# First block's gates: eight of sixteen column blocks computed with the tokens stationary, then turned

## The chip, the cores and the metric

The kernel runs on one core of one Trainium2 chip. The metric is device time in microseconds for one launch, as the median of several runs. The times shown were taken on one chip, and the profile is one further execution on it.

## The reference, cut to what matters

Two transformer blocks follow each other on a sequence of 256 tokens with 2048 features, in float32. The change touches the gate of the first block's attention.

```python
def swa_sink_mixer(h, w_in, sinks):
    q, k, v, z = split(h @ w_in, [2048, 2304, 2560])   # 2048 | 256 | 256 | 2048 columns
    ...                                               # windowed attention with sinks, 32 heads of 64
    return o, z

def first_block(x, ...):
    h = rmsnorm(x, g_pre)
    o, z = swa_sink_mixer(h, w_in_a, sinks_a)
    y = (o * silu(z)) @ w_out_a
    return x + rmsnorm(y, g_post)

def second_block(x, ...):      # MLA and differential attention, a merge, an FFN, three norms
    ...
```

The gate is `silu(z)`, with z the last 2048 columns of `h @ w_in_a`.

## The kernel before, in words

**Weights.** All matrices are cut into 128 x 128 tiles and stored in the order in which they are used, 16 tiles to a chunk of 1 MB. `Weights.load` (L54) fetches a chunk on SyncE's queue into one of four `w_raw` buffers. `Weights.cut` splits 8 tiles at a time into a high part `w_hi` (ScalarE, L85) and a low part `w_lo` (VectorE, L86), each with four buffers. A product is the sum hi·hi + hi·lo + lo·hi.

**Two ways of multiplying.** `gemm` (L330) takes one block of 128 output columns. The weight tile is stationary. For each of the 16 tiles along the 2048 features there is one matmul of the high weights with the activation's high and low halves side by side (512 columns moving), and one of the low weights with the high half (256 columns moving). The result has features on the partitions and tokens along the free axis. `gemm_nat` (L389) takes 512 output columns, four weight tiles at a time. A block of 128 tokens is stationary, and the weights move: for each of the 16 steps and each of two token blocks there are three matmuls of 512 columns. The result has tokens on the partitions.

**Turning.** Where a result with tokens on the partitions is wanted with features there, `turned` (L450) has VectorE transpose 32 x 32 blocks (L453), and `moved` (L441) then issues 16 DMAs of 16 KB (L446) that bring the blocks to their partitions, from GpSimd's queue (POOL) unless told otherwise. Weights are stored with columns permuted (`_quarters`) so that this works out.

**First block.** K and V are computed first, then 16 blocks of queries by `gemm`, then 16 blocks of gates, each a `gemm` (L640 to L650). A gate block j becomes `g[j]` in these steps: total on ScalarE and VectorE (L419, L212), times the norm's factor (L212), tanh (ScalarE, L646), z(1 + tanh) (VectorE, L647), 0.5 of it times the attention's output `o_a` (VectorE, L636), and the split into halves (ScalarE, L245, and VectorE, L246). The output projection `out_a` follows: three runs of `gemm_nat` (L681), which take `g[0]`, `g[1]`, ... in order, and four blocks one at a time.

**Attention beside it.** The 16 pairs of heads are worked on beside these products by generators in `between`, an `Interleave`. After every 8 weight tiles it has a tick, and each tick lets one generator go on to its next `yield`; a generator names how many ticks it waits. The first active one that is due goes first, and a queued one starts only when no active one is due. `attention_a` uses two ticks in three: at one it issues the values of pair i - 3 (`values_a`, on PE, with a bank `ps_t`) and the scores of pair i (`ps_s`), and two ticks later the transposes and DMA moves of the probabilities (`turned_probs`: twelve pieces on POOL, four on SyncE, `prob_t<-prob_tr`). Afterwards it has one free tick in three. Between the program's order and the engines' own order stands a scheduler that places instructions of each engine, so that weight cuts run ahead of the matmuls.

After `out_a`, a norm over its result (`rstd` on POOL, L708) stands between the first block and the second.

Of the kernel before, what the change touches and what calls it, by code (L numbers as in the profile page):

```python
# [10 lines left out]
F32R = mybir.dt.float32r  # L11
AF = mybir.ActivationFunctionType
ALU = mybir.AluOpType

P = 128
# [156 lines left out]
def block_kernel(ctx, tc, order, w, x01, xt, bc, rw, cst, out):  # L172
    nc = tc.nc
# [11 lines left out]
    between = Interleave()  # L185

    def unit(name, dt=F32):
        return up.tile([P, 512], dt, name=name, tag="u", bufs=NU)
# [7 lines left out]
    def sm(name, n=4):  # L196
        return small.tile([P, n], F32, name=name, tag="sm", bufs=16)

    def bank(tag):
        return psum.tile([P, 512], F32, name=f"ps_{tag}", tag=tag, bufs={"g": 4, "s": 2, "t": 2}[tag])  # L200

    def half(t, i):
        return t[:, (i % 2) * S:(i % 2) * S + S]
# [37 lines left out]
    def split_scaled(src, g, hl):  # L241

        hi = hl[:, 0:S]
        if g is None:
            a = nc.scalar.copy(out=hi, in_=src)  # L245
            b = nc.vector.tensor_tensor(out=hl[:, S:], in0=src, in1=hi.bitcast(F32), op=ALU.subtract)  # L246
        else:
            a = nc.scalar.activation(out=hi, in_=src, func=AF.Copy, scale=g)
            b = nc.vector.scalar_tensor_tensor(out=hl[:, S:], in0=src, scalar=g, in1=hi.bitcast(F32),
                                               op0=ALU.mult, op1=ALU.subtract)  # L250
        return a, b
# [78 lines left out]
    def gemm(name, m, acts, tag="g"):  # L330

        ps = bank(tag)
        parts = [(ps, W.take(name, k * P, m * P), acts[k]) for k in range(len(acts))]
        if len(parts) > HALF:
            runs(parts[:HALF], parts[HALF:], HALF)
        else:
            runs(parts, [], len(parts))
        return ps
# [19 lines left out]
    def gemm_sum(name, m, acts):  # L358

        kind[0] = "hi"  # L360
        ps = bank("g")
        n = len(acts)
        for k in range(n):
            hi, lo = W.take(name, k * P, m * P)
            mm(ps[:, 0:S], hi, acts[k][:, 0:S], k == 0, False)
            mm(ps[:, 0:S], hi, acts[k][:, S:], False, False)
            mm(ps[:, 0:S], lo, acts[k][:, 0:S], False, k == n - 1)
            between.tiles(1)
        return ps
# [31 lines left out]
    def gemm_nats(name, cols, acts, late):  # L401

        banks = [[bank("g") for _ in range(2)] for _ in cols]
        n = len(acts)
        kind[0] = "hi"
        for ks in (range(late), range(late, n)):
            for col, pp in zip(cols, banks):
                for k in ks:
                    while acts[k] is None:
                        between.tick()  # L410
                    hi, lo = W.take(name, k * P, col, 4)
                    for tb in range(2):
                        nat3(pp[tb], acts[k], tb, hi, lo, k == 0, k == n - 1)
                    between.tiles(4)
        return banks
# [6 lines left out]
    def scaled(o, ps, rb):  # L422
        total(o, ps)
        tt(o, o, rb, ALU.mult)
# [71 lines left out]
    h = Lazy(KD, first_h)  # L496
# [8 lines left out]
    for k in range(KD):  # L505
        if k % 2 == 0:
            h.upto(k + 4)
        parts = [(ps_k[j], W.take("in_a", k * P, D + j * P), h[k]) for j in range(2)]
# [9 lines left out]
    r_a = const.tile([P, 2], F32, name="r_a")  # L518
# [80 lines left out]
    done = set()  # L599
    between.every, between.apart = 4, 1  # L600
    between.add(first_norm())
    o_a = []
    early = []
    for j in range(16):
        ps = gemm("in_a", j, h, "s" if j == 2 else "g")
# [7 lines left out]
        for i, b in early:  # L613
            if i % 2 == 0:
                q, o = unit("q_a"), unit("o_a")
# [10 lines left out]
                            axis=mybir.AxisListType.X)  # L626
# [2 lines left out]
    tt(neglam, dots[:, 1:2], dots[:, 0:1], ALU.subtract)  # L629
    nc.vector.tensor_scalar(out=neglam, in0=neglam, scalar1=0.2, scalar2=None, op0=ALU.subtract)  # L630

    g = []

    def gate_a(j, z):
        hl = unit(f"g{j}", F32R)
        nc.vector.scalar_tensor_tensor(out=z, in0=z, scalar=0.5, in1=half(o_a[j // 2], j), op0=ALU.mult, op1=ALU.mult)  # L636
        split_scaled(z, None, hl)
        g.append(hl)

    for j in range(16):  # L640
        ps = gemm("in_a", 20 + j, h)
        if j % 2 == 0:
            z2, th2 = unit("z"), unit("th")
        z, th = half(z2, j), half(th2, j)
        scaled(z, ps, rb)
        nc.scalar.activation(out=th, in_=z, func=AF.Tanh, scale=0.5)  # L646
        nc.vector.scalar_tensor_tensor(out=z, in0=th, scalar=1.0, in1=z, op0=ALU.add, op1=ALU.mult)  # L647
        while j not in done:
            between.tick()
        gate_a(j, z)  # L650
    between.drain()


# [25 lines left out]
    for i in range(3):  # L679
        parts = []  # L680
# [9 lines left out]
    for m in range(12, 15):  # L690
        ps = gemm("out_a", m, g)
        t = y[m]
# [3 lines left out]
    t = sm("ms_y", 2)  # L696
    for tb in range(2):
        nc.vector.tensor_reduce(out=t[:, tb:tb + 1], in_=sums_y[:, 3 * tb:3 * tb + 3], op=ALU.add,
                                axis=mybir.AxisListType.X)
    nc.vector.tensor_scalar(out=t, in0=t, scalar1=1.0 / D, scalar2=EPS, op0=ALU.mult, op1=ALU.add)  # L700
    ps = gemm_sum("out_a", 15, g)
# [31 lines left out]
    h = Lazy(KD, second_h)  # L733
# [53 lines left out]
    ps = gemm("kpe", 0, h)  # L787
# [71 lines left out]
    for u in range(4):  # L859
        kn = []  # L860
        for i in range(4):
            ps = gemm("uk", 4 * u + i, ckv)
# [9 lines left out]
        for tb in range(2):  # L872
            t = unit("v_m")
# [6 lines left out]
        for i in range(4):  # L880
            ps = gemm("uq", 4 * u + i, cq)
# [140 lines left out]
    for u in range(4):  # L1022
        qk = []
        for c in (0, 16):
            parts = []
            for tb, ps in enumerate(gemm_nat("dqk", (c + 4 * u) * P, h)):
                z = unit("qk_d")
# [8 lines left out]
        for tb in range(2):  # L1036
# [3 lines left out]
                                           op0=ALU.mult, op1=ALU.subtract)  # L1040
# [24 lines left out]
    pairs = gemm_nats("diff", [0, 512], y_d, 8)  # L1065
# [11 lines left out]
    h = [None] * KD  # L1077
# [20 lines left out]
    for tb in range(2):  # L1098
        nc.vector.tensor_reduce(out=ms[:, tb:tb + 1], in_=sums3[:, 4 * tb:4 * tb + 4], op=ALU.add,
                                axis=mybir.AxisListType.X)  # L1100
# [5 lines left out]
    for u in range(KF // 4):  # L1106
# [5 lines left out]
        parts = []  # L1112
        for tb, ps in enumerate(pg):
            z = unit("ffn")
# [21 lines left out]
    for cb in range(3):  # L1136
        for tb, ps in enumerate(gemm_nat("down", cb * 512, act)):
            residual(cb, tb, ps)
            t = x2n[2 * cb + tb]
# [12 lines left out]
    for tb in range(2):  # L1152
        nc.vector.tensor_reduce(out=ms3[:, tb:tb + 1], in_=tot[:, 5 * tb:5 * tb + 3], op=ALU.add,
                                axis=mybir.AxisListType.X)
# [3 lines left out]
    for tb in range(2):  # L1158
        parts = [(slice(0, 512), pp[0])]
        if tb:  # L1160
            parts = [(slice(0, 256), bank("s")), (slice(256, 512), bank("s"))]
        for i, (cols, ps) in enumerate(parts):
# [3 lines left out]
            if i + 1 < len(parts):  # L1166
                nc.vector.scalar_tensor_tensor(out=ms3[:, tb:tb + 1], in0=tot[:, 5 * tb + 3:5 * tb + 4],
                                               scalar=1.0 / D, in1=ms3[:, tb:tb + 1], op0=ALU.mult, op1=ALU.add)
        r = sm("rms", 1)
        nc.scalar.activation(out=r, in_=tot[:, 5 * tb + 2 + len(parts):5 * tb + 3 + len(parts)], func=AF.Sqrt,  # L1170
                             scale=1.0 / D, bias=ms3[:, tb:tb + 1])
        nc.vector.reciprocal(out=r, in_=r)
        for cb in range(4):
            t = x2n[2 * cb + tb]
# [35 lines left out]
def _quarters(n):  # L1210

    return np.arange(n).reshape(-1, 4, 4, 32).transpose(0, 2, 1, 3).reshape(-1)
# [6 lines left out]
def _matrices(i):  # L1219

    pairs = []
    for j in range(16):
        kt = j // 8
        for hd in (16 * kt + j % 8, 16 * kt + 8 + j % 8):
            pairs.extend(range(hd * 64, hd * 64 + 64))
    pairs = np.array(pairs)
    in_a, in_2 = i["w_in_a"][0], i["w_in_2"][0]
    uq = i["w_uq_2"][0].reshape(768, 16, 192)
    ukv = i["w_ukv_2"][0].reshape(512, 16, 256)
    kpe = in_2[:, 1280:1344]  # L1230
    ffn = np.concatenate([i["w_ffn_gate_2"][0], i["w_ffn_up_2"][0]], axis=1)[:, _quarters(2 * DFF)]
    return {
        "in_a": np.concatenate([in_a[:, :2048][:, pairs], in_a[:, 2048:2560], in_a[:, 2560:][:, pairs]], axis=1),
        "out_a": i["w_out_a"][0][pairs][:, np.concatenate([_quarters(1536), np.arange(1536, 2048)])],
        "in_2": in_2[:, :1280],
        "kpe": np.concatenate([kpe, kpe], axis=1),
        "dqk": in_2[:, 1344:5440][:, _quarters(2 * D)],
        "dv": in_2[:, 5440:7488],
        "gate": in_2[:, 7488:][:, _quarters(2 * D)],
        "uq": np.concatenate([uq[:, :, :128].reshape(768, -1), uq[:, :, 128:].reshape(768, -1)], axis=1),  # L1240
        "uk": ukv[:, :, :128].reshape(512, -1),
        "uv": ukv[:, :, 128:].reshape(512, -1),
        "mla": i["w_mla_proj_2"][0][:, _quarters(D)],
        "diff": i["w_diff_proj_2"][0][:, _quarters(D)],
        "out": i["w_out_2"][0][:, _quarters(D)],
        "ffn": ffn,
        "down": i["w_ffn_down_2"][0][:, _quarters(D)],
    }
# [36 lines left out]
```

## Time and profile before

| | us |
|---|---|
| median of 3 runs | 1968.07 (1968.05 to 1968.17) |
| profiled execution | 1968.4 |
| its span in the trace | 1966.6 |
| gates: first matmul to the start of `out_a` | 134.7 to 239.75 |
| three `gemm_nat` runs of `out_a` | 239.75 to 305.0 |
| PE busy over the span | 1954.7 (99%) |
| VectorE busy | 1227.4 (62%) |
| ScalarE busy | 1009.2 (51%) |
| POOL busy | 636.4 (32%) |

PE is the matrix engine's matmuls, PEld its weight loads, DVE is VectorE, ACT is ScalarE, POOL is GpSimd, SP is SyncE. L12 is line 12 of the kernel. A row of a tile's view gives an instruction with its count, then the shortest, the median and the longest duration in ns, then when the first and the last of them start. A row of the chain or the timeline gives the start and the duration in us. The idle time in front of an instruction stands in brackets with what ended it.

### The profile page before, as it was taken

To read this page: it belongs to the slowest core of one execution; us is meant where nothing else is said; L and a number is where in the kernel's file an instruction comes from. 1 tells how busy PE (TensorE), PEld (TensorE's weight loads), DVE (VectorE), ACT (ScalarE), POOL (GpSimd) and SP (SyncE) were. 2 spreads that over 40 slices of the span, in tenths; PEclk is the share of its full clock that TensorE was granted. 3 is DMA by queue.
4 is the path that set the end of the run, shared out by engine and by line. 5 is a ranking of instruction groups with operands and counts; after the bars stand their busy time and mean duration, and the time that the engine had idled before them with its cause. 6 is when DMAs were issued, how large, how long until landed. Compare 5 with 4: busy or idle time off the path is not lost.

```text
span 1966.6 us, 27298 instructions
## 1 busy us (share of the span) xinstructions
PE 1954.7 (99%) x9404; PEld 1631.3 (83%) x9404; DVE 1227.4 (62%) x1897; ACT 1009.2 (51%) x1588; POOL 636.4 (32%) x1291
## 2 busy tenths in 40 slices
PE   9999999999999999999999999999999999999998
PEld 8888888888888888888888888888888888888887
DVE  7889855888756655556666566655555555545454
ACT  6677655756545544455564344544444444444443
POOL 0555244013362532445622455323332222220000
PEclk9999999999999999999999999999999999999999
DMA  8565565445565665656566665655665555565553
GB/s 306 186 207 198 188 224 182 171 158 178 192 210 191 211 222 203 215 193 216 189 234 217 211 212 194 245 206 192 209 223 206 201 205 203 204 224 193 193 192 107
DMA packets 114491, 398.94 MB, mean 203 GB/s; under 512 B 32880, under 2 KB 66288, under 8 KB 71216
## 3 DMA queue, kind: packets, MB, share of 16 engines
q1 hardware_dynamic: 72096, 370.24, 53.3%
q0 software_dynamic: 41104, 24.99, 4.7%
q10 hardware_dynamic: 1152, 1.97, 0.3%
q8 instruction: 74, 1.21, 0.2%
q14 instruction: 65, 0.53, 0.1%
HBM read 364.03 MB, written 2.10 MB: 186 GB/s over the span
## 4 chain that ended last, share of the span: by engine, by line
PE 95%; DMA 2%; issue 1%; DVE 1%; POOL 1%; ACT 0%; DVEq 0%; POOLq 0%
PE ps_g L209 90%; PE ps_s L209 4%; DMA turned<-turn 2%; PE ps_t L209 2%; POOL turned L446 0%; PE ps_warm L230 0%; DVE w_lo L86 0%; DVE rope_t L212 0%; POOL rstd L290 0%; ACT x1n L1181 0%; DVE q_r L212 0%; DVE y L719 0%; DVE y L718 0%; POOL rstd L708 0%; DVE turn L453 0%
## 5 line engine op out<-in xcount | busy, mean ns | idle before, releaser
L86 DVE TENSOR_TENSOR w_lo<-w_raw,w_hi 128x1024 fp32r<-128x1024 f32 (+1 forms) x677 | 821.8, 1217 | 622.5 <-ACT w_hi L85 619.2
L85 ACT CAST w_hi<-w_raw 128x1024 fp32r<-128x1024 f32 (+1 forms) x677 | 707.4, 1048 | 772.0 <-PE ps_g L209 743.4
L446 POOL DMA_DIRECT2D turned<-turn x744 | 365.3, 498 | 618.6 <-DVE turn L453 339.0
L209 PE MATMUL ps_g<-w_hi,t_lo 128*128 128x512 f32 x1176 | 457.6, 389 | 0.0
L209 PE MATMUL ps_g<-w_lo,t_hi 128*128 128x512 f32 x1176 | 457.5, 389 | 0.0
L209 PE MATMUL ps_g<-w_hi,t_hi 128*128 128x512 f32 x1176 | 457.5, 389 | 0.0
L209 PE MATMUL ps_g<-w_hi,h 128*128 128x512 f32 x1280 | 400.6, 391 | 0.0
L209 PEld LDWEIGHTS ps_g<-w_hi,h 128*128 128x128 f32 x1280 | 240.4, 188 | 50.5 <-issue 0.3
L209 PEld LDWEIGHTS ps_g<-w_hi,t_lo 128*128 128x128 f32 x1176 | 220.8, 188 | 46.0 <-DVE t_lo L212 0.3
L209 PEld LDWEIGHTS ps_g<-w_lo,t_hi 128*128 128x128 f32 x1176 | 220.8, 188 | 45.9
L209 PEld LDWEIGHTS ps_g<-w_hi,t_hi 128*128 128x128 f32 x1176 | 220.8, 188 | 45.6
L209 PE MATMUL ps_g<-w_lo,h 128*128 128x512 f32 x640 | 249.1, 389 | 0.0
L446 POOL DMA_DIRECT2D prob_t<-prob_tr x336 | 165.3, 500 | 199.8 <-DVE prob_tr L461 105.3
L209 PE MATMUL ps_g<-h,w_hi 128*128 128x512 f32 x648 | 160.0, 394 | 0.0
L209 PEld LDWEIGHTS ps_g<-w_lo,h 128*128 128x128 f32 x640 | 120.2, 188 | 24.4
L209 PEld LDWEIGHTS ps_g<-h,w_hi 128*128 128x128 f32 x648 | 117.9, 188 | 25.5 <-issue 2.3
L209 PEld LDWEIGHTS ps_g<-h,w_lo 128*128 128x128 f32 x648 | 84.7, 191 | 7.0 <-issue 2.7
L209 PE MATMUL ps_g<-h,w_lo 128*128 128x256 f32 x648 | 88.2, 284 | 0.0
L209 PE MATMUL ps_g<-w_hi,y_m 128*128 128x512 f32 x256 | 80.0, 391 | 0.0
L209 PE MATMUL ps_g<-w_hi,y_d 128*128 128x512 f32 x256 | 79.0, 389 | 0.0
L446 POOL DMA_DIRECT2D x1n<-turn x96 | 47.1, 498 | 89.9 <-DVE turn L1016 41.8
L290 POOL TENSOR_TENSOR rstd<-ms,mhalf 128x2 f32<-128x2 f32 (+1 forms) x9 | 7.7, 852 | 167.4 <-DVE ms L285 151.5
(250 smaller groups left out, 1838.1 us busy)
## 6 DMA issues: line engine op xcount, KB each, us to landing
w_raw<-w SPq DMA_DIRECT2D x337, 1024.0 KB, 5.0
turned<-turn POOLq DMA_DIRECT2D x744, 16.0 KB, 3.8
prob_t<-prob_tr POOLq DMA_DIRECT2D x336, 24.0 KB, 3.6
turned<-turn SPq DMA_DIRECT2D x216, 16.0 KB, 2.1
row<-rw SPq DMA_DIRECT2D x12, 256.0 KB, 5.1
prob_t<-prob_tr SPq DMA_DIRECT2D x112, 24.0 KB, 2.9
w_raw<-w SPq DMA_DIRECT2D x5, 512.0 KB, 7.4
x_t<-xt SPq DMA_DIRECT2D x7, 256.0 KB, 7.4
```

The lines of the kernel that those rows point to most:

```text
L85: a = nc.scalar.copy(out=hi[:, q], in_=src[:, q])
L86: b = nc.vector.tensor_tensor(out=lo[:, q], in0=src[:, q], in1=hi.bitcast(F32)[:, q], op=ALU.subtract)
L209: nc.tensor.matmul(out=o, lhsT=a, rhs=b, start=start, stop=stop, skip_group_check=True)
L290: nc.gpsimd.tensor_tensor(out=r, in0=t, in1=mhalf[:, 0:n], op=ALU.pow)
L446: (fourth if fourth and a == 3 else queue).dma_start(out=o[32 * b:32 * b + 32, a * n:a * n + n], in_=tr[32 * a:32 * a + 32, b * n:b * n + n])
```

## The change

The first 8 of the 16 gate blocks are computed as two runs of `gemm_nat`, 512 columns each. For each run and each of the two token blocks, ScalarE scales the bank by the norm's factor, which is now one number per partition, and takes the tanh; VectorE forms z(1 + tanh); then the 128 x 512 result is turned. The 16 DMAs of the first token block go to POOL and those of the second to SyncE. A new generator `gate_a`, one per run, is put into `between`: it waits 13 ticks, then multiplies with `o_a` and splits, two blocks to a tick. Gate blocks 8 to 15 stay as they were. The gate columns of these 1024 are stored permuted.

```diff
-    g = []
-    def gate_a(j, z):
-        hl = unit(f"g{j}", F32R)
-        nc.vector.scalar_tensor_tensor(out=z, in0=z, scalar=0.5, in1=half(o_a[j // 2], j), op0=ALU.mult, op1=ALU.mult)
-        split_scaled(z, None, hl)
-        g.append(hl)
-    for j in range(16):
+    g = [None] * 16
+    def split_g(j, z):
+        g[j] = unit(f"g{j}", F32R)
+        split_scaled(z, None, g[j])
+    def gate_a(i, parts):
+        yield 13
+        for m in range(4):
+            j = 4 * i + m
+            while j not in done:
+                yield
+            if m % 2 == 0:
+                z2 = unit("z")
+            for tb, t in enumerate(parts):
+                q = slice(tb * P, tb * P + P)
+                nc.vector.scalar_tensor_tensor(
+                    out=half(z2, j)[:, q].rearrange("p (a i) -> p a i", a=4),
+                    in0=t.rearrange("p (a g i) -> p g a i", a=4, g=4)[:, m], scalar=0.5,
+                    in1=half(o_a[j // 2], j)[:, q].rearrange("p (a i) -> p a i", a=4), op0=ALU.mult, op1=ALU.mult)
+            split_g(j, half(z2, j))
+            if m % 2:
+                yield
+    for i in range(2):
+        parts = []
+        for tb, ps in enumerate(gemm_nat("in_a", (20 + 4 * i) * P, h)):
+            z, th = unit("z"), unit("th")
+            nc.scalar.activation(out=z, in_=ps, func=AF.Copy, scale=r_a[:, tb:tb + 1])
+            nc.scalar.activation(out=th, in_=z, func=AF.Tanh, scale=0.5)
+            nc.vector.scalar_tensor_tensor(out=z, in0=th, scalar=1.0, in1=z, op0=ALU.add, op1=ALU.mult)
+            parts.append(turned(z, nc.sync if tb else nc.gpsimd))
+        between.add(gate_a(i, parts))
+    for j in range(8, 16):
         ps = gemm("in_a", 20 + j, h)
...
         while j not in done:
             between.tick()
-        gate_a(j, z)
+        nc.vector.scalar_tensor_tensor(out=z, in0=z, scalar=0.5, in1=half(o_a[j // 2], j), op0=ALU.mult, op1=ALU.mult)
+        split_g(j, z)
     between.drain()
```

More of the change, by code (lines that the diff above doesn't have):

```diff
@@ L1232, in _matrices @@
     return {
-        "in_a": np.concatenate([in_a[:, :2048][:, pairs], in_a[:, 2048:2560], in_a[:, 2560:][:, pairs]], axis=1),
+        "in_a": np.concatenate([in_a[:, :2048][:, pairs], in_a[:, 2048:2560],
+                                in_a[:, 2560:][:, pairs][:, np.concatenate([_quarters(1024), np.arange(1024, 2048)])]], axis=1),
         "out_a": i["w_out_a"][0][pairs][:, np.concatenate([_quarters(1536), np.arange(1536, 2048)])],
```

## The prediction

> **What bounds the kernel now.** I read the page's totals first, then the busy times of the stretch that changes, then the chain of waits inside it.
>
> ```profile
> span 1966.6 us, 27298 instructions
> PE 1954.7 (99%) x9404; PEld 1631.3 (83%) x9404; DVE 1227.4 (62%) x1897; ACT 1009.2 (51%) x1588; POOL 636.4 (32%) x1291
> ...
> core 0: us, PE busy (x) PEld busy (x) DVE busy (x) ACT busy (x) POOL busy (x), PEclk, DMA share, GB/s
> 134.70:239.75 105.05, 105.05 (x650) 87.11 (x649) 91.04 (x228) 74.03 (x181) 47.09 (x96) 1.00 0.57 191
> 239.75:305.00 65.25, 65.25 (x290) 54.04 (x289) 38.97 (x42) 34.92 (x52) 30.60 (x63) 1.00 0.65 229
> ```
>
> PE covers 1954.7 of 1966.6 us, and every microsecond of the gates (134.7 to 239.75) and of the three runs behind them, at the full granted clock. VectorE follows with 91.04 of 105.05 us (87%) in the gates. So time is gained here only by making PE's own sequence shorter, and lost by making PE wait. The whole kernel has 1966.6 - 1954.7 = 11.9 us in which PE isn't busy, so nothing that only removes waits can bring more than that.
>
> The chain shows what a gate block costs PE, the run behind it what the other form costs:
>
> ```profile
> 191.29 9.44 PE ps_g L209 x48
> 200.72 0.80 PE ps_t L209 x8
> 201.53 0.85 PE ps_s L209 x8
> 202.38 7.67 PE ps_g L209 x48
> ...
> L209 PE MATMUL ps_g<-w_hi,g x192: 389/389/396, 239.8 to 304.8; 128*128 128x512 f32 x192
> L209 PE MATMUL ps_g<-w_lo,g x96: 389/389/397, 240.0 to 304.6; 128*128 128x512 f32 x96
> ```
>
> A gate block by `gemm` is 16 tiles x 2 = 32 matmuls. The two stretches of 48 between attention's entries hold 96 matmuls, three blocks, in 9.44 + 7.67 = 17.11 us: 5.70 us a block, 22.81 us for four. The three runs of `gemm_nat` in `out_a` are 192 + 96 = 288 matmuls in the 65.25 us of the window above: 227 ns each, 21.75 us for a run of 512 columns with the same 16 steps.
>
> **The change part by part, and the sum.**
>
> *PE.* Two runs replace eight blocks: 2 x (22.81 - 21.75) = 2.1 us less. The two forms stream the same columns (16 x 4 x 768 against 16 x 6 x 512), so the whole gain is in the overhead of the 256-column matmuls and of 128 weight loads against 96. Attention's entries (0.80 + 0.85 us) are the same number at the same ticks: a run has 16 x 4 tiles, eight ticks, as four blocks have.
>
> [...]
>
> *VectorE and ScalarE.* What a block costs them now, and the nearest rows for the new forms:
>
> ```profile
> L419 ACT COPY z<-ps_g x16: 347/360/374, 143.6 to 240.0; 128x256 f32<-128x256 f32 x16
> L212 DVE TENSOR_TENSOR z<-z,ps_g x16: 387/412/422, 144.1 to 241.3; 128x256 f32<-128x256 f32 x16
> L212 DVE TENSOR_TENSOR z<-z,rb_a x16: 407/424/426, 144.6 to 241.7; 128x256 f32<-128x256 f32 x16
> L646 ACT ACTIVATE th<-z x16: 402/417/418, 145.3 to 242.2; 128x256 f32<-128x256 f32 x16
> L647 DVE SCALAR_TENSOR_TENSOR z<-th,z x16: 377/424/428, 145.9 to 242.6; 128x256 f32<-128x256 f32 x16
> L636 DVE SCALAR_TENSOR_TENSOR z<-z,o_a x16: 376/424/426, 146.7 to 243.1; 128x256 f32<-128x256 f32 x16
> L245 ACT CAST g<-z x16: 397/402/408, 147.9 to 243.7; 128x256 fp32r<-128x256 f32 x16
> L246 DVE TENSOR_TENSOR g<-z,g x16: 409/416/427, 149.3 to 245.0; 128x256 fp32r<-128x256 f32 x16
> ...
> L212 DVE TENSOR_TENSOR x2g<-x1n,row x8: 648/680/684, 1191.9 to 1243.2; 128x512 f32<-128x512 f32 x8
> L1086 ACT ACTIVATE x2g<-x1n x8: 622/626/628, 1192.1 to 1243.8; 128x512 f32<-128x512 f32 x8
> L453 DVE STREAM_TRANSPOSE turn<-x2g x8: 702/703/705, 1193.6 to 1245.1; 128x512 f32<-128x512 f32 x8
> L989 DVE SCALAR_TENSOR_TENSOR y_d<-o_t,g_d,y_d x32: 339/346/353, 681.9 to 1072.0; 128x128 fp32r<-128x128 f32 x32
> ```
>
> Four blocks cost VectorE 4 x (412 + 424 + 424 + 424 + 416) = 8.4 us and ScalarE 4 x (360 + 417 + 402) = 4.7 us. A run costs VectorE 2 x 0.68 for z(1 + tanh), 2 x 0.703 for the transposes, 8 x 0.346 for the products with `o_a` (now 128 columns each) and 4 x 0.416 for the low halves: 7.2 us. ScalarE has 4 x 0.626 + 4 x 0.402 = 4.1 us. Both become 1.2 and 0.6 us lighter a run. PE didn't wait for them, so this counts as nothing; it pays for the faster pace at which weights must be cut.
>
> *The moves on POOL.* Each run adds 16 pieces to POOL:
>
> ```profile
> L446 POOL DMA_DIRECT2D turned<-turn x744: 496/498/551, 262.8 to 1734.7; - x186
> L446 SPq DMA_DIRECT2D turned<-turn x216: 507/588/1637, 541.4 to 1724.6; - x108
> ...
> 160.82 3.44 POOL L446 DMA_DIRECT2D prob_t<-prob_tr  x7 [7.60 <-PE ps_t L209]
> 166.83 7.39 POOL L446 DMA_DIRECT2D prob_t<-prob_tr  x15 [2.57 <-issue]
> 176.36 0.99 POOL L446 DMA_DIRECT2D prob_t<-prob_tr  x2 [2.14 <-DMA prob_t<-prob_tr]
> ...
> prob_t<-prob_tr POOLq DMA_DIRECT2D x336, 24.0 KB, 3.6
> ...
> DMA to landing us min/median/max: 1.6/3.4/6.0
> ...
> 189.63 0.80 PE ps_t L209 x8
> ```
>
> 16 x 0.498 = 8.0 us a run. The first run's result is turned about 163 us (the run ends near 160, then copy, tanh, product and transpose, 2.6 us). POOL then holds the 24 pieces of pairs 10 and 11. If the 16 come in front of pair 11's, the three lots are 40 x 0.498 + 2.57 + 2.14 = 24.6 us from 160.8, so issued at 185.4 and landed 3.6 us later, at 189.0. The values of pair 11 stand at 189.63 now and come some 1.6 us earlier with the gain up to there, at 188.0. PE would wait 1.0 us. If the 16 come behind, PE waits for nothing, as the gate needs them only 13 ticks later. I take half, 0.5 us. The second run is turned near 185 to 190; pairs 13 to 15 have POOL idle between them, so it costs nothing. Without that idle time it would cost what the first one may. The ends for the range: zero, and 1.0 + 6.0 - 3.6 = 3.4 us if landing takes the 6.0 us that the last row but one has as the longest in this stretch.
>
> *The moves on SyncE.* 16 x 0.588 = 9.4 us a run, in the queue that also loads weights:
>
> ```profile
> 1213.20 10.96 SPq L446 DMA_DIRECT2D turned<-turn  x16
> 1224.26 18.73 SPq L54 DMA_DIRECT2D w_raw<-w  x6
> ...
> w_raw<-w SPq DMA_DIRECT2D x337, 1024.0 KB, 5.0
> ...
> L86 DVE TENSOR_TENSOR w_lo<-w_raw,w_hi 128x1024 fp32r<-128x1024 f32 (+1 forms) x677 | 821.8, 1217 | 622.5 <-ACT w_hi L85 619.2
> ...
> SPq L446 <- DVE prob_tr L461: 32.3, 13, 7.5
> ```
>
> A chunk lasts PE 16 x 0.340 = 5.4 us. A load is released when the chunk four earlier is cut, three chunks or 16.3 us ahead of need, less 5.0 us of landing: 11.3 us in reserve. Of the four split buffers three are cut ahead, 24 tiles or 8.2 us more. A lot of 9.4 us, with the worst wait that SyncE had for a transpose (7.5 us) ahead of it, holds loads for 16.9 us, inside 19.5 us. Lots of 16 on this queue at 1213.20 cost PE no wait. I count nothing.
>
> *The gates' end.* `out_a` takes `g[k]` every 65.25 / 48 = 1.36 us, so `g[4]` 5.4 us after its start, `g[6]` 8.2, `g[7]` 9.5. Counting ticks from the program (attention free at one in three, then 13 ticks), the second `gate_a` makes `g[4]` and `g[5]` half-way through the last block, and `g[6]` and `g[7]` after it. Now `g[15]` starts its last step at 245.0, 5.3 us behind the start. Were `g[6]` and `g[7]` wholly behind that, four products, two casts and two subtractions (4 x 0.346 + 2 x 0.402 + 2 x 0.416 = 3.0 us) would end 8.7 us after the start: 0.5 us late for `g[6]`, and 1.7 with a weight cut of 1.2 us (the row of `w_lo` above) between. But they wait for nothing that PE is still making and fit into VectorE's gaps of that chain. I count nothing.
>
> *Behind it.* The norm after `out_a` stands on POOL behind `out_a`'s pieces:
>
> ```profile
> 328.79 0.16 DVE L706 SCALAR_TENSOR_TENSOR ms_y<-ps_t,ms_y 128x2 f32<-128x2 f32 x1 [2.58 <-PE ps_t L209]
> ...
> 327.44 2.94 POOL L446 DMA_DIRECT2D turned<-turn  x6 [3.35 <-DMA turned<-turn]
> 330.40 0.73 POOL L708 TENSOR_TENSOR rstd<-ms_y,mhalf 128x2 f32<-128x2 f32 x1
> ```
>
> Its input is there at 328.95, and it starts at 330.40: 1.45 us may go or double as the pieces shift against PE. They start from PE's results and shift with it; I count nothing and keep 1.5 us either way.
>
> Sum: -2.1 + 0.5 = -1.6 us. The profiled execution has 1968.4 us, 0.3 over the median; against that execution it would be 1966.8, against the median of 1968.07 it is 1966.5.
>
> **Rivals.** [...]
>
> *Waits eat the gain*: POOL's lots in front of attention's pieces and the late gates together cost 2 to 4 us: 1968 to 1970. For it: the 1.0 us and 0.5 us margins above are thin. Against it: the light load of the remaining queue and the generator's late due time.
>
> *Slower, by the weights*: SyncE's lots hold chunk loads past the reserve. It decides from 19.5 us of hold; each microsecond beyond costs PE one, at two places. At 23 us of hold it gives 2 x 3.5 - 2.1 = +4.9, 1973. For it: VectorE at 87% makes transposes late, and loads behind them wait in order. Against it: 16.9 us as the worst that rows give.
>
> *Faster than the sum*: POOL's 1.45 us also goes, and no wait appears: 1968.07 - 3.5 = 1964.5.
>
> **How the numbers follow.** 0.2% is 3.9 us, about what a measurement of this kernel can tell from no change; it puts the bounds at 1964.1 and 1972.0. Chances: my forecast with its own range (1965.5 to 1967.3) 0.56; faster than the sum 0.15, of which 0.05 past 1964.1; waits eat the gain 0.15; no gain on PE 0.07; slower by the weights 0.07. So faster 0.05, same 0.88, slower 0.07. The range of 1964.2 to 1969.8 leaves out the slower case (0.07), what lies past 1964.1 (0.05) and the upper tail of the waits (0.03): 0.15. Its upper end is the sum with 3.4 us at POOL and 0.5 at the gates' end, 1969.9.
>
> **What would show it.** Right: matmuls `h` by `w_hi` at 227 ns in the gates, `out_a` starting some 1.6 to 2.1 us earlier, and no wait of PE for `prob_t`, `g` or `w_lo`. Wrong: a wait of PE on `ps_t` for a DMA near pair 11 or 13 (POOL), on `g` at 243 to 248 us (the gates' end), or for `w_lo` with ScalarE waiting for a `w_raw` DMA (SyncE); or an unchanged length of the gates with PE busy throughout.

## The result and the profile after

The changed kernel takes 1973.30 us (median, 1970.45 to 1976.96), the kernel before 1967.72 us (1967.25 to 1968.26): a ratio of 1.0028 with a 95% interval of 1.0019 to 1.0036. It is slower, by 5.6 us; 1966.5 had been predicted, with 1969.8 as the upper end. The profiled execution has 1972.59 us, 4.2 us over that of the kernel before.

The totals of the changed kernel's page, and the busy times of stretches of it (columns as before: busy time and count for each engine, then granted clock, DMA share, GB/s):

```profile
span 1970.8 us, 27230 instructions
...
PE 1957.4 (99%) x9340; PEld 1630.1 (83%) x9340; DVE 1225.5 (62%) x1889; ACT 1012.2 (51%) x1580; POOL 652.2 (33%) x1323
```

```profile
135.07:245.03 109.96, 106.89 (x586) 85.00 (x585) 86.25 (x211) 72.62 (x169) 63.01 (x128) 0.98 0.57 188
...
215.00:225.00 10.00, 6.93 (x40) 5.70 (x39) 8.43 (x21) 4.29 (x9) 6.90 (x14) 0.92 0.90 321
225.00:230.00 5.00, 5.00 (x23) 4.12 (x22) 1.40 (x2) 2.49 (x6) 0.52 (x2) 0.81 0.11 30
...
330.00:345.00 15.00, 14.44 (x85) 12.77 (x84) 8.54 (x24) 6.85 (x18) 4.07 (x8) 0.89 0.19 51
```

The first row is the gates, from their first matmul to the start of `out_a`: 109.96 us, where the kernel before has 105.05. They were meant to become shorter and are 4.9 us longer. PE is idle for 3.07 us of them, and the clock, 1.00 over the gates before, is 0.92 and 0.81 in the two stretches that follow each other at 215 us.

PE's waits in the changed kernel (in all, times, longest) name what it was idle for, and PE's timeline shows the place:

```profile
PE ps_t L209 <- DMA prob_t<-prob_tr: 3.1, 1, 3.1
...
PE ps_t L209 <- DVE diag L297: 0.6, 1, 0.6
```

```profile
214.21 3.82 PE L209 MATMUL ps_g<-h,w_hi 128*128 128x512 f32 x16
217.87 2.07 PE L209 MATMUL ps_g<-h,w_lo 128*128 128x256 f32 x16
223.01 1.11 PE L209 MATMUL ps_t<-prob_t,v_a 128*64 128x256 f32 x8 [3.07 <-DMA prob_t<-prob_tr]
224.05 5.26 PE L209 MATMUL ps_g<-h,w_hi 128*128 128x512 f32 x16
```

The same 16 matmuls right behind the values of a pair, in the kernel before:

```profile
210.78 3.92 PE L209 MATMUL ps_g<-h,w_hi 128*128 128x512 f32 x16
```

The values of attention pair 14 wait 3.07 us for the moves of its probabilities. The 16 matmuls behind them take 5.26 us where 3.92 are usual at such a place, and the eight of the values 1.11 us where others take 0.87: the clock costs 1.34 + 0.24 = 1.6 us more. No row names `g` or `w_hi` as late; `w_lo` has 0.3 us, at 420.9 us, and as much in the kernel before.

Why the moves are late is read on POOL's timeline, of the kernel before in two rows, then of the changed one, and on the chain of the same stretch in the changed one:

```profile
191.39 3.43 POOL L446 DMA_DIRECT2D prob_t<-prob_tr  x7 [0.35 <-DMA prob_t<-prob_tr]
201.66 5.88 POOL L446 DMA_DIRECT2D prob_t<-prob_tr  x12 [6.83 <-PE ps_t L209]
```

```profile
165.21 2.46 POOL L446 DMA_DIRECT2D prob_t<-prob_tr  x5 [2.58 <-issue]
169.29 6.85 POOL L446 DMA_DIRECT2D turned<-turn  x14 [1.63 <-ACT w_hi L85]
177.56 0.99 POOL L446 DMA_DIRECT2D turned<-turn  x2 [1.41 <-DMA turned<-turn]
178.71 12.08 POOL L446 DMA_DIRECT2D prob_t<-prob_tr  x24 [0.16 <-issue]
192.49 0.99 POOL L446 DMA_DIRECT2D prob_t<-prob_tr  x2 [1.70 <-DMA prob_t<-prob_tr]
...
199.49 2.11 POOL L446 DMA_DIRECT2D prob_t<-prob_tr  x4 [1.83 <-DMA prob_t<-prob_tr]
201.59 7.83 POOL L446 DMA_DIRECT2D turned<-turn  x16
209.42 4.48 POOL L446 DMA_DIRECT2D prob_t<-prob_tr  x9
215.35 0.50 POOL L446 DMA_DIRECT2D prob_t<-prob_tr  x1 [1.46 <-DMA prob_t<-prob_tr]
```

```profile
201.60 6.93 POOL turned L446 x15
...
209.43 0.97 POOL prob_t L446 x2
210.40 6.13 DMA prob_t<-prob_tr
216.53 0.28 issue
216.80 5.48 DMA prob_t<-prob_tr
222.29 0.72 issue
223.01 1.11 PE ps_t L209 x8
```

The two rows `turned<-turn` x14 and x2 are the first run's lot of moves, x16 the second's. Counting twelve pieces to a pair, the 24 pieces at 178.71 are pairs 11 and 12, those from 192.49 to 201.60 are pair 13, and those from 209.42 are pair 14. The second lot begins the moment pair 13 is issued, and pair 14 begins the moment the lot is issued. In the kernel before pair 14 was issued from 201.66 on, after 6.83 us without work. Here it starts 7.8 us later, its pieces take 5.5 to 6.1 us to land instead of the median of 3.4, and the last landing comes at 222.3, while PE was ready at 219.9.

### The profile page after: what moved, and what is told of

The parts are those of the page before. It is cut to its first block, busy times and chain, and to the rows that moved or that the text cites. A ratio compares the mean times of both kernels' runs of the same rounds, so it can differ in the third digit from the quotient of the medians.

```text
span 1970.8 us, 27230 instructions
## 1 busy us (share of the span) xinstructions
PE 1957.4 (99%) x9340; PEld 1630.1 (83%) x9340; DVE 1225.5 (62%) x1889; ACT 1012.2 (51%) x1580; POOL 652.2 (33%) x1323
## 4 chain that ended last, share of the span: by engine, by line
PE 96%; DMA 1%; issue 1%; POOL 1%; DVE 1%; ACT 0%; SPq 0%; POOLq 0%; DVEq 0%
PE ps_g L209 90%; PE ps_s L209 4%; PE ps_t L209 2%; DMA prob_t<-prob_tr 1%; POOL turned L446 0%; DVE w_lo L86 0%; DMA w_raw<-w 0%; POOL prob_t L446 0%; DVE rope_t L212 0%; POOL rstd L290 0%; ACT w_hi L85 0%; DVE prob L430 0%; ACT x1n L1208 0%; DVE q_r L212 0%; ACT bias L556 0%
## 5 line engine op out<-in xcount | busy, mean ns | idle before, releaser
L85 ACT CAST w_hi<-w_raw 128x1024 fp32r<-128x1024 f32 (+1 forms) x677 | 709.6, 1051 | 786.2 <-PE ps_g L209 758.5
L446 POOL DMA_DIRECT2D turned<-turn x776 | 381.0, 498 | 612.2 <-DVE turn L453 314.5
L209 PE MATMUL ps_g<-w_hi,h 128*128 128x512 f32 x1408 | 441.6, 391 | 0.0
L209 PEld LDWEIGHTS ps_g<-w_hi,h 128*128 128x128 f32 x1408 | 264.3, 188 | 57.1 <-issue 1.7
L209 PE MATMUL ps_g<-w_lo,h 128*128 128x512 f32 x704 | 274.1, 389 | 0.0
L209 PEld LDWEIGHTS ps_g<-w_lo,h 128*128 128x128 f32 x704 | 132.2, 188 | 26.7
L209 PE MATMUL ps_g<-h,w_hi 128*128 128x512 f32 x520 | 130.9, 397 | 0.4 <-DVE h L249 0.4
L209 PEld LDWEIGHTS ps_g<-h,w_hi 128*128 128x128 f32 x520 | 95.3, 190 | 21.3 <-issue 2.7
L209 PEld LDWEIGHTS ps_g<-h,w_lo 128*128 128x128 f32 x520 | 68.5, 191 | 6.0 <-issue 2.0
L209 PE MATMUL ps_g<-h,w_lo 128*128 128x256 f32 x520 | 71.5, 284 | 0.0
```

Of the source, the lines that this page charges most:

```text
L85: a = nc.scalar.copy(out=hi[:, q], in_=src[:, q])
L209: nc.tensor.matmul(out=o, lhsT=a, rhs=b, start=start, stop=stop, skip_group_check=True)
L446: (fourth if fourth and a == 3 else queue).dma_start(out=o[32 * b:32 * b + 32, a * n:a * n + n], in_=tr[32 * a:32 * a + 32, b * n:b * n + n])
```

## The experiments

The theory: the second lot, issued from 201.59 us on, stands in front of pair 14 on POOL (from 209.42, with the first lot's delay still in the queue) and makes PE wait, and the clock adds to it. Against it stood a cause on SyncE (its lots bunch weight loads and slow all landings), a cause in the matmuls themselves (the new form with attention's entries between), and plain size (one run is harmless, two are not). Each ratio is to the kernel before, timed beside it.

**One run instead of two (e1).**

```diff
-    for i in range(2):
+    for i in range(1):
...
-    for j in range(8, 16):
+    for j in range(4, 16):
```

> Only blocks 0 to 3 go over to the new form; blocks 4 to 15 stay. Backlog theory (the 16 moves of a lot stand on POOL in front of attention's pieces, the second lot meets the delay that the first one left, pair 14's probabilities land late, PE waits 3.1 us and then runs at a lower clock): with one lot POOL has 8 us less and catches up, no wait of PE for a move of probabilities, and the PE gain is half of what both runs bring, 0.5 us: 0.2 to 1.0 us under the kernel before. Rival (the lot on SyncE holds the weight loads, which then come in a bunch and slow the landing of the pieces): the one lot on SyncE is over by 185 us, a bunch follows near 190, and a wait of PE would show at pair 12 or 13, 1 to 3 us slower than before.

1968.50 us against 1968.18, ratio 1.0003 (0.9994 to 1.0012). PE has no wait for `prob_t`. So the first run and its lots cost nothing that shows, and the loss belongs to the second, or to both together. The gain of 0.2 to 1.0 us that had been expected is neither shown nor excluded.

**No moves (e2).** The 64 moves are left out, and the gate reads the transposed blocks where they lie.

```diff
-            parts.append(turned(z, nc.sync if tb else nc.gpsimd))
+            tr = unit("turn")
+            nc.vector.transpose(out=tr, in_=z)
+            parts.append(tr)
```

> The 64 moves are left out (the gates take the transposed blocks where they lie, so part of the computation is missing); matmuls, copies, transposes and products are all there. What is left is PE's own gain. The prediction's 2.1 us would give 2.1 us under the kernel before. My count after seeing the trace, which takes attention's entries out of the blocks as well (5.58 us a block, 21.85 a run), gives 1.0 us; with the norm's 1.4 us wait on POOL gone too, up to 2.4. No wait of PE for probabilities by either theory. Slower than before only if VectorE or the order of the scores costs by itself (then 0 to 1 us slower).

1966.79 us against 1968.18, ratio 0.9994 (0.9985 to 1.0003). Its trace prices the matmuls alone, with PE busy throughout:

```profile
134.90:239.10 104.20, 104.20 (x587) 83.45 (x585) 86.29 (x211) 72.34 (x169) 47.00 (x96) 1.00 0.56 188
```

The gates last 104.20 us where they lasted 105.05: the new form brings 0.85 us, not 2.1, and it is the 64 moves that turn this into a loss.

**All lots on SyncE (e3), and all on POOL (e4).**

```diff
-            parts.append(turned(z, nc.sync if tb else nc.gpsimd))
+            parts.append(turned(z, nc.sync))        # e3; nc.gpsimd in e4
```

> All four lots on SyncE's queue, 32 pieces a run, none on POOL. Backlog theory: POOL is as in the kernel before, no wait of PE for probabilities, 0.5 to 2 us faster than before. Rival (loads held on SyncE): loads are held about 19 us a run, twice as long; the bunch is larger, pieces land later or weights come late, and the time is at or over that of the changed kernel (5 us over before or more).

> All four lots on POOL, 32 pieces a run (16 us), SyncE's queue as before. Backlog theory: POOL's delay doubles, several pairs from 11 to 15 are late, PE waits 6 to 15 us in all and runs at a lower clock after each wait: 8 to 18 us slower than before. Rival (loads held on SyncE): loads are regular again, pieces land sooner, and the time is under that of the changed kernel, 0 to 4 us over before.

Both are much slower: 1988.92 us, ratio 1.0102 (1.0089 to 1.0116), for SyncE and 1990.35, ratio 1.0106 (1.0090 to 1.0121), for POOL. With all on POOL, PE waits 12.9 us for `prob_t` at two places. With all on SyncE it waits 13.3 us for `prob_t`, and 2.9 for `w_hi`. SyncE's queue, and PE at the longer of the two waits:

```profile
198.68 21.56 SPq L446 DMA_DIRECT2D turned<-turn  x32
220.62 2.40 SPq L446 DMA_DIRECT2D prob_t<-prob_tr  x4
```

```profile
224.60 1.55 PE L209 MATMUL ps_t<-prob_t,v_a 128*64 128x256 f32 x8 [9.63 <-DMA prob_t<-prob_tr]
229.66 3.78 PE L209 MATMUL ps_g<-h,w_hi 128*128 128x512 f32 x8 [2.90 <-ACT w_hi L85]
```

The four pieces of a pair that go by SyncE stand behind 32 moves, at 0.67 us each, and PE waits for them. So the order against attention's pieces decides on either queue; the weights come second (2.90 us). The theory missed both times: it had put e3 at 0.5 to 2 us faster, without the four pieces of each pair that SyncE issues, and e4 at 8 to 18 us slower, where it is 22. Which of the two queues did it in the changed kernel these two runs don't tell.

**Two runs, but later (e5)**: blocks 8 to 15 are computed in the new form, in the order blocks 0 to 5, the two runs, blocks 6 and 7, and the gate's generator waits 5 ticks instead of 13.

```diff
+    for j in range(6):
+        block(j)
-    for i in range(2):
+    for i in range(2, 4):
...
+    for j in range(6, 8):
+        block(j)
```

> The same two runs, but for blocks 8 to 15 and placed later: blocks 0 to 5 one by one, then the two runs, then blocks 6 and 7; gate_a waits 5 ticks in place of 13. The lots come near 200 and 225 us, and attention's last pieces stand near 215 on POOL, so the first lot meets one pair and the second none. Backlog theory: PE waits for no move of probabilities, the PE gain of 1.0 us stands, with the 1.4 us of the norm's wait perhaps gone too: 0.5 to 2.5 us faster than before. Rival (holding the loads on SyncE and the bunch behind it is enough to make PE wait): the same 22 us of lots stand on SyncE, so 2 us or more slower than before, with weights late.

1967.38 us against 1967.96, ratio 0.9998 (0.9989 to 1.0006). A lot of 16 at 209.96 stands in front of pair 15's pieces at 219.86, and PE waits once, where the theory had expected no wait:

```profile
230.78 0.87 PE L209 MATMUL ps_t<-prob_t,v_a 128*64 128x256 f32 x8 [1.71 <-DMA prob_t<-prob_tr]
231.58 2.18 PE L209 MATMUL ps_g<-h,w_lo 128*128 128x256 f32 x16
```

Here the matmuls behind the wait keep their 0.87 and 2.18 us: this wait of 1.71 us cost only itself.

**Moves in small portions (e6).** The gate's generator issues the moves, four pieces on POOL and four on SyncE at each of four steps, so that attention's pieces come between.

```diff
-        yield 13
+        yield 1
+        parts = [unit("turned") for _ in trs]
+        for a in range(4):
+            for tb, (tr, o) in enumerate(zip(trs, parts)):
+                for b in range(4):
+                    (nc.sync if tb else nc.gpsimd).dma_start(...)
+            yield 4 if a == 3 else 1
```

> The same as the changed kernel, but the moves are issued by the generator, in four steps of 4 pieces on POOL and 4 on SyncE with a tick or more between, so they come behind attention's pieces where these are due (the second run's all come behind the last pair on POOL). The number of pieces and the queues are the same. Backlog theory: what counts is the order on the queues, no wait of PE for probabilities, 0 to 2.5 us faster than before, or up to 2 us slower if the second run's gates now come too late for the projection (a wait of PE on g near 245 us). If the pieces themselves cost (DMA engines, contention), it stays near the changed kernel, 4 us or more over before.

1966.78 us against 1967.96, ratio 0.9994 (0.9985 to 1.0003). No wait for `prob_t`. On POOL nine pieces of the first lot go ahead of pair 12 and seven behind it; the second run's come from 218.14 on, behind pair 15. The same 64 moves as in the changed kernel then cost nothing.

**Only POOL's lots (e7), and only SyncE's (e8).** In the first, the second token block is used as transposed, without its moves; in the second, the first.

```diff
-            parts.append(turned(z, nc.sync if tb else nc.gpsimd))
+            tr = unit("turn")
+            nc.vector.transpose(out=tr, in_=z)
+            parts.append(moved(tr, unit("turned"), nc.gpsimd) if tb == 0 else tr)   # e7
+            parts.append(moved(tr, unit("turned"), nc.sync) if tb == 1 else tr)     # e8
```

> The changed kernel with the moves of the second token block (SyncE's lots) left out: its transposed blocks are used where they lie. POOL's lots stand as in the changed kernel, and SyncE's queue is as before the change. If POOL's backlog alone makes pair 14 late, PE waits 2 to 4 us there as in the changed kernel and the time is 4 to 6 us over before. If the bunch of loads behind SyncE's lots is needed (pieces landed in 6.1 and 5.5 us while the DMA engines were 0.90 busy), there is no wait and the time is 0 to 2 us under before.

> The changed kernel with the moves of the first token block (POOL's lots) left out in the same way; SyncE's lots stay. Backlog theory with POOL as the queue that decides: no wait of PE, 0 to 2 us under before. If SyncE's lots alone suffice, through the four pieces of each pair that stand behind them or through the loads, PE waits at pair 13 or 14, 2 us or more over before.

With POOL's lots alone the loss is all there: 1973.66 us against 1967.96, ratio 1.0029 (1.0018 to 1.0041); its profiled execution is the slowest of the six, with 1976.71. With SyncE's alone it is gone: 1968.67, ratio 1.0002 (0.9993 to 1.0011). PE's timeline of the first, and PE's window where SyncE's lots alone bunch the loads:

```profile
192.88 1.55 PE L209 MATMUL ps_t<-prob_t,v_a 128*64 128x256 f32 x8 [2.49 <-DMA prob_t<-prob_tr]
194.36 1.65 PE L209 MATMUL ps_s<-k_a,q_a 64*128 64x128 f32 x8
...
225.27 0.87 PE L209 MATMUL ps_t<-prob_t,v_a 128*64 128x256 f32 x8 [2.01 <-DMA prob_t<-prob_tr]
226.07 5.53 PE L209 MATMUL ps_g<-h,w_hi 128*128 128x512 f32 x16
```

```profile
215.00:225.00 10.00, 10.00 (x59) 8.39 (x59) 9.24 (x23) 6.13 (x14) 5.53 (x12) 1.00 0.81 286
```

At 192.88 it is pair 11, behind the first lot, at 225.27 pair 14, behind the second. With SyncE's lots alone the DMA engines are as crowded at 215 us (0.81; 0.90 in the changed kernel) and PE doesn't wait. The crowd from SyncE is not needed for the loss and doesn't make it by itself.

**The second lot behind the last pair (e9).** Everything of the change stays; only the POOL lot of the second run is issued by its generator, five ticks later.

```diff
-        yield 13
+        if i:
+            yield 5
+            parts[0] = moved(parts[0], unit("turned"), nc.gpsimd)
+            yield 8
+        else:
+            yield 13
```

> The changed kernel with one difference: the second run's lot on POOL is issued by its generator, after a wait of 5 ticks, and so stands behind the last pair's pieces on POOL. The first lot and both lots on SyncE stay. Backlog theory: the 7.8 us in front of pair 14 are gone, pair 14's pieces go out near 204 us and land before 215, PE waits for no move of probabilities (or under 1 us at pair 11), 0 to 2 us faster than before the change; the second run's gates come later by some 15 us, and a wait of PE on g under 2 us is possible. If the first lot, the loads held on SyncE or VectorE's order make pair 14 late instead, the wait of 3 us and the 5 us over before stay.

1966.53 us against 1968.10, ratio 0.9992 (0.9983 to 1.0001), while the changed kernel stood at 1.0028. POOL's timeline and the shares of the chain from 180 to 245 us:

```profile
202.88 5.87 POOL L446 DMA_DIRECT2D prob_t<-prob_tr  x12 [1.73 <-DMA turned<-turn]
211.77 3.91 POOL L446 DMA_DIRECT2D prob_t<-prob_tr  x8 [3.03 <-DVE prob_tr L461]
217.70 1.96 POOL L446 DMA_DIRECT2D prob_t<-prob_tr  x4 [2.02 <-DMA prob_t<-prob_tr]
219.65 1.12 POOL L446 DMA_DIRECT2D turned<-turn  x2
```

```profile
by line: PE ps_g L209 88.9%; PE ps_t L209 7.4%; PE ps_s L209 4.0%
```

Pair 14 is issued at 202.88 instead of 209.42, the lot from 219.65 on behind pair 15, and the chain of this stretch is PE alone. This one edit takes the whole loss away: the wait, the lowered clock behind it, and also a split of pair 15's scores on PE (next section), which stand together here.

**The lots alone (e10).** The kernel before, with two lots that nobody reads, after blocks 3 and 7; its matmuls are as they were.

```diff
+        if j in (3, 7):
+            turned(z2)
```

> The kernel before with two lots of moves added and nothing else: after blocks 3 and 7 the tile z is transposed and moved once more, 16 pieces on POOL each, and no one reads the result. All matmuls are as before. Backlog theory: the lots come in front of attention's pieces as in the changed kernel, pair 14 or 15 is late, PE waits 1 to 5 us and loses up to 2 us by a lower clock: 2 to 7 us slower than before. If the new form of the matmuls (its evacuation on ScalarE, the order of the scores) is needed for the loss: no wait, within 1 us of before.

1974.30 us against 1968.10, ratio 1.0033 (1.0020 to 1.0045). PE's longest wait:

```profile
192.56 0.87 PE L209 MATMUL ps_t<-prob_t,v_a 128*64 128x256 f32 x8 [2.44 <-DMA prob_t<-prob_tr]
```

Two lots on POOL cost as much without the new form of the matmuls as with it. But the wait is at pair 11, behind the first lot, and not at pair 14 or 15 as expected; ahead of pair 14 PE is idle for 0.68 us, and the trace names no DMA there. So this run shows that lots in front of attention's pieces are enough for such a loss, and not that the second one does it; for that there are e1 and e9.

**Three runs (e11)**, with the lots of the second and third behind the last pair, to see whether more is to be had.

```diff
-            yield 5
+            yield (5, 1)[i - 1]
             parts[0] = moved(parts[0], unit("turned"), nc.gpsimd)
-            yield 8
+            yield (8, 3)[i - 1]
...
-    for i in range(2):
+    for i in range(3):
```

> The changed kernel with three runs of 512 (blocks 0 to 11) in the new form instead of two; the GpSimd moves of the second and the third run are issued behind those of the last attention pair, SyncE's where they fall. Theory (GpSimd's order against the attention pairs made the changed kernel slow, and a run of 512 gives TensorE some 0.5 us): no wait for a pair's values, a further 0.5 us off the gates, 1 to 3 us faster than before (about 1966). Rival (three are too many: the third run's blocks come late for the next layer's product, or SyncE's third lot holds weights): TensorE waits on the gates' tile or on weights after the last attention matmul, 0 to 4 us slower than before (1968 to 1972).

1976.28 us against 1968.12, ratio 1.0040 (1.0026 to 1.0053): the rival, and 8 us where it allowed 4. No wait for `prob_t`, but POOL issues the two lots until 237.9, and the eight blocks of the second and third run are cast only from 246.8 to 252.1 us. PE, through with the first run's four blocks, waits for the next. PE's timeline there, and its windows:

```profile
250.22 0.79 PE L209 MATMUL ps_g<-w_hi,g 128*128 128x512 f32 x1 [3.02 <-ACT g L245]
250.81 0.63 PE L209 MATMUL ps_g<-w_lo,g 128*128 128x512 f32 x1
...
256.94 0.62 PE L209 MATMUL ps_g<-w_hi,g 128*128 128x512 f32 x2
```

```profile
245.00:250.00 5.00, 2.19 (x11) 1.51 (x9) 4.57 (x15) 2.09 (x6) 0.00 (x0) 0.92 0.55 202
250.00:255.00 5.00, 4.78 (x11) 3.80 (x12) 2.46 (x9) 1.38 (x4) 0.00 (x0) 0.50 0.14 54
```

A matmul that takes 0.39 us elsewhere takes 0.79, at a clock of 0.50 for 5 us. Behind `out_a` PE waits another 2.3 us for `h`, where the kernel before has 0.3. So with the lots placed like this a third run loses more than it brings; another placing was not tried.

## Why the prediction was wrong

**The moves on POOL: the step that failed.** The prediction put it thus: "The second run is turned near 185 to 190; pairs 13 to 15 have POOL idle between them, so it costs nothing." The 16 pieces were priced rightly as POOL's time (7.83 us for the second lot, 8.0 predicted), but two things of their place were not. First, the idle time was read from the trace of before as if it stayed. The first lot began at 169.29 and not at 163, with ScalarE's weight cut as the last thing ahead of it, and pushed pairs 11 to 13 back: pair 13 was issued until 201.60, where before it was done by 194.8. The 6.83 us ahead of pair 14 were spent before the second lot came. Second, POOL stops between pieces, and its timeline names earlier moves that have yet to land: pair 13 takes 9.1 us for twelve pieces, half as much again as 12 x 0.498. The cause is shown by e9, where moving this one lot removes the wait, by e1, where the first lot alone makes none, and by e7 and e8, where POOL's lots alone have the loss and SyncE's alone have not. "Without that idle time it would cost what the first one may" stood beside the step, with 3.4 us as its upper end; 3.07 us of waiting lies inside it. The rival "waits eat the gain" had this mechanism too, with a chance of 0.15, but a time of 1968 to 1970.

*The first lot* was given 0.5 us, half of the 1.0 at pair 11. It did come in front of pair 11's pieces, and the changed kernel's trace has no wait there: POOL issues the 24 pieces at 178.71 without a stop. In e7, with the same order on POOL, it stops within them, and pair 11 waits 2.49 us. So that nothing came of this term in the profiled execution is in part luck.

**The price of a wait.** The prediction counted PE's wait once. In the changed kernel it cost more: its gates are 3.1 us idle and lose 1.6 to the clock. Another 1.1 us is in the scores of pair 15, which the scheduler put on PE as two halves around three other matmuls:

```profile
200.04 0.92 PE L209 MATMUL ps_s<-k_a,q_a 64*128 64x128 f32 x4
200.89 0.97 PE L209 MATMUL ps_g<-h,w_hi 128*128 128x512 f32 x3
201.79 0.92 PE L209 MATMUL ps_s<-k_a,q_a 64*128 64x128 f32 x4
```

Four take as long as eight do elsewhere (0.93), so 0.9 more, and 0.2 for one more entry (below). With 0.9 gained, 3.1 + 1.6 + 1.1 - 0.9 makes 4.9, as the trace has it. The split doesn't come from the wait: e1 and e8 have one and no wait for `prob_t`, at ratios of 1.0003 and 1.0002, where e2, e6 and e9, without it, are at 0.9994, 0.9994 and 0.9992. What makes the scheduler split them is not shown. The clock, the split and the 1.2 us that PE's gain fell short are what took the time past the upper end of the range.

**PE's gain: right in sign, under half in size.** 2.1 us were taken, 0.85 came (e2). The 22.81 us for four blocks came from two stretches that each stand behind an entry of attention; the 21.75 us for a run from `out_a`, which has no such entries. In the kernel before, matmuls next to an entry are slower: the 16 of 512 columns take 3.94 us behind one (at 150.38 us), 3.82 elsewhere (at 143.06). With e for this cost per entry, the two stretches give a block as (17.11 - 2e)/3, and the whole gates of before, with seven entries of 1.65 us and three of 0.80, as (105.05 - 13.95 - 10e)/16; both agree at e = 0.2 us, with a block at 5.57, four at 22.3. Read directly, from start to start away from entries, a block is 3.66 us of high weights (143.06 to 146.72) and 1.91 of low ones (154.16 to 156.07), 5.57 too. A run of the changed kernel is (52.9 - 5 x (1.66 + 0.2))/2 = 21.8 us between 135.07 and 188.0. The gain is some 0.45 us a run, where 1.06 had been taken. An estimated 0.3 of it is the shape of the 64 matmuls with 256 columns that a run does without: by the two readings above one takes 119 ns, and half of one with 512 takes 114. What the fewer weight loads bring is not shown.

**The moves on SyncE: right.** A lot lasts 11.04 us on its queue in the changed kernel (9.4 predicted), and PE waits for no weight in the gates. e8, where the same holds, shows the lots harmless. The bound of 19.5 us no run measures: with 32 pieces in a row (e3), 21.56 us, PE waits 2.90 us for `w_hi`, but it had stood still for 9.63 us just before, and the first 32 pieces there, 20.75 us, cost no wait for a weight. The rival "slower, by the weights" gave about the time that came, 1973, but by a mechanism that isn't in the trace.

**The gates' end: right for two runs.** No wait on `g` in the changed kernel. With a third run (e11) it is the wait that decides.

**VectorE: right; ScalarE: not.** VectorE's total is 1.9 us lower, 2.4 predicted. ScalarE's is 3.0 higher, where 1.2 less was expected; its weight cuts alone went from 707.4 to 709.6 us. Neither bounds anything here.

**The norm behind it.** It was left at nothing, with 1.5 us either way. PE's wait for `diag` falls from 1.94 to 0.56 us in the changed kernel and in most of the variants, but in the changed kernel the eight matmuls of 512 columns behind it take 3.76 us where the kernel before has 2.20, at a lowered clock. The product that follows starts 4.9 us late (339.50 against 334.56), and the span ends 4.2 us late; where the other 0.8 us are saved stays open. e9's profiled span, 1965.0, is 1.6 us under that of before, which is the predicted sum by luck: 0.9 come from the gates, and the rest from behind the norm, by a term that the prediction didn't have.

## What to carry to other kernels

Idle time of a queue may be spent once. When two lots of work are put into it, replay the queue with the first lot in place, each item at its own release, before asking what the second costs; and look at which item with a deadline stands directly behind the new lot. Where a lot has time to spare, issue it behind the item that hasn't: here the same 16 DMAs five ticks later are worth 0.36% (ratios of 1.0028 and 0.9992), some 1.1 us of it by the scores that are no longer split.

## What was not expected of the hardware

Six waits of PE, of 2.01 to 3.65 us, were followed by matmuls at a lower clock: after 3.07 us (changed kernel) 1.6 us more; after 2.49 us (e7) 1.55 and 1.65 instead of 0.87 and 0.93, 1.4 more, and after 2.01 us (e7) 5.53 instead of 3.92, 1.6 more; after 2.44 us (e10) 1.62 and 4.84 instead of 0.93 and 3.94, 1.6 more; after 3.65 us (e3) 1.57 and 3.07 instead of 0.93 and 2.17, 1.5 more; after 3.02 us (e11) 0.79 instead of 0.39, and longer matmuls for some 5.7 us. After 1.71 us (e5) nothing: the clock is 1.00 from 225 to 235 us. In the changed kernel the granted clock is 1.00 up to 223.50 us, 0.50 for the next 3.41 us and 1.00 again, and once more 0.50 for 3.41 us from 336.14 on, 112.64 us or 33 such lengths behind the first time. The windows of e7 give 3.4 us at 0.50 for each of its two waits, those of e11 6.8. In the 3.41 us just ahead of the lowered clock PE was idle for 2.9 us in the changed kernel (busy for 0.49), for 2.1 and 2.0 in e7, 2.4 in e10 and 2.1 in e11, the last four estimated from the places that the windows give for the drop.

The changed kernel's runs spread over 6.5 us, the slowest (1976.96) at a mean clock of 0.996 and the fastest (1970.45) at 0.999, so the same program loses more to the clock in some executions than in others; only one has a trace, so whether its waits differ too is not shown. In the norm's stretch (330 to 345 us) the clock is 0.89 in the changed kernel and 0.90 in e9, and 1.00 before, although PE's pause there is shorter than before. In the changed kernel the 3.41 us ahead of the lowered clock hold matmuls of 1 and of 128 columns beside the pause of 0.56 us. What lowers the clock there is not shown, nor what makes POOL wait within a lot for landings of its own (1.46 us at 215.35 in the changed kernel).
